# FFN up projections: one 512-column product of the high weights with both parts of the activation

## The chip, the cores and the metric

The kernel runs on one core of a Trainium2 chip, as one program in one launch. The metric is device time in microseconds (us) from start to end of that program. TensorE (PE in the profile) multiplies, VectorE (DVE) and ScalarE (ACT) do the elementwise work, and SyncE (SP) issues the DMA transfers. TensorE reads SBUF and writes PSUM, a memory of eight banks that hold 512 float32 columns each.

## What is computed

Two blocks over 256 tokens of 1024 features, all in float32. The first block has two layers, one with an mLSTM mixer and one with causal attention, each followed by a convolutional feed-forward net (FFN) with 2816 hidden features. The second block has two layers of convolution and sparse attention. The change lies in the FFN, which runs twice:

```
def conv_ffn(x, norm_g, w_up, conv_w, conv_b, w_down):
    u = rmsnorm(x, norm_g) @ w_up                 # 1024 -> 2 * 2816
    up = jnp.pad(u, ((0, 0), (CONV_W - 1, 0), (0, 0)))
    c = conv_b + up[:, 0:s_] * conv_w[0]
    for j in range(1, CONV_W):                    # 3 taps over the tokens
        c = c + up[:, j:j + s_] * conv_w[j]
    val, gate = jnp.split(c, 2, axis=-1)
    return (jax.nn.silu(gate) * val) @ w_down
```

## The kernel before

**Split products.** A float32 operand is split exactly into a high and a low part: ACT writes the high part (line 435), DVE subtracts it to get the low part (line 448). A product of two split operands is three matmul passes into the same PSUM columns: high by high (line 569), high by low (line 570), low by high (line 571). The first operand of a pass is stationary, 128x128 weights that are loaded ahead of the pass; the second is streamed through, one column per token.

**The FFN.** The hidden features go in 22 chunks of 128, each with a value half and a gate half. `up(j)` reads a 1 MB chunk of up weights (two loads of 512 KB) and computes, with features on the partitions, two blocks of 128x256: `gemm_pair` puts them in the two halves of one PSUM bank, 8 contraction steps of three passes each. For the first two chunks (HEAD) the products start from activations without the norm's factor. Then ACT scales each block from PSUM with the last tap, DVE adds the other two taps (two SCALAR_TENSOR_TENSOR each, also reading PSUM), ACT takes the silu of the gate, DVE multiplies, and the result is split again. `down(j - 2)` follows `up(j)` in the program; it takes 24 passes of 256 columns in the first FFN, and 12 of 512 columns (activation stationary, weights streamed) in the second. Four PSUM banks hold the down sums for the whole FFN; the other four serve everything else.

**Other work in the FFNs.** The modulation of the second block (`ada`) is a matrix-vector product on DVE: 48 chunks of 512 KB, each one SCALAR_TENSOR_TENSOR over 128x1024 with an accumulator (line 453). It is spread in the program over 38 of the 44 chunks.

**The order.** All instructions are recorded in program order. A planner in the kernel then goes through time with its own table of durations and fixes the order of each engine: the first in the program among those that are ready and whose buffers have room. On the chip each engine works through its list in that order. Buffers come from pages: 24 pages R of 1024 columns for split operands (a weight part takes a whole page, an activation part a quarter), 25 pages F for the rest.

**The convolution's mean in the second block.** In each layer of it, four small matmuls (line 1237) sum the taps, ACT copies the sums, and they go to DRAM and back through DMA (`zscr`, lines 1242 and 1244). TensorE then has a product of that result with the constant `ones` in its list (124 rows, line 422), and what stands behind it waits.

Of the kernel before, what the change touches and what calls it, by code (L numbers as in the profile page):

```python
# [20 lines left out]
EPS = 1e-6  # L21
# [20 lines left out]
for _n, _c in CONSTS:  # L42
# [4 lines left out]
# pages of on-chip memory: name -> (columns, dtype, count)  # L47
PAGES = {
    "R": (1024, F32R, 24),
# [4 lines left out]
# buffers: name -> (page, part of a page, columns)  # L54
POOLS = {
    "w": ("R", 4, 1024),
    "r": ("R", 1, 256),
# [10 lines left out]
SLOT_LAT = 200.0  # L68
WARM = 4096 / 1.2
# [23 lines left out]
class Buf:  # L93
    """A slot of a pool from its first to its last use, or a tile of its own (ap given)."""
# [41 lines left out]

class Op:
# [3 lines left out]
class Program:  # L141
    """Records the kernel's instructions in order, then fixes the order in which each engine issues its own:
    the first in the program among those whose operands and buffers are ready."""
# [39 lines left out]
    @staticmethod  # L183
    def spread(ops, p0, p1):
        """Gives ops the priorities of the program's positions p0..p1."""
        for i, op in enumerate(ops):
            op.prio = p0 + (p1 - p0) * (i + 0.5) / len(ops)

    def order(self, slots):
        """slots: page name -> list of tiles. Returns the ops in the planned order, with table loads."""  # L190
# [30 lines left out]
        # the place for a buffer: an opened page with the least room if it is a small one, else a whole page  # L221
# [54 lines left out]
        while left:  # L276
# [43 lines left out]
            for b in op.new:  # L320
# [7 lines left out]
                o = o * 256 if size < 4 else 0  # L328
# [53 lines left out]
def build(ctx, tc, a):  # L382
# [57 lines left out]
    # has the activation table ready for what comes after x  # L440
# [70 lines left out]
    # the part of FIRST that begins at each of n columns, then of the next  # L511
# [7 lines left out]
    hold = [None]  # L519

    def split_w(raw, n):
        hi, lo = new("w", n), new("w", n)
        op = act(hi, raw, AF.Copy)
        if hold[0]:
            pg.after(op, hold[0])
        tt(lo, raw, hi.f32, ALU.subtract)
        return hi, lo

    class Chunk:
        """k blocks k0..k1 of a chunk of weights; split, or as it is (native) for a float32 product; cuts: in pieces."""  # L530

        def __init__(self, dram, kc, mc, k0=0, native=False, cuts=None):
            self.mc, self.kp, self.k0 = mc, 1024 // mc, k0
            self.parts = []
            for k in range(k0, kc, self.kp):
                n = min(self.kp, kc - k) * mc
                raw = new("raw", n)
                if cuts:
                    hi, lo = new("w", n), new("w", n)
                    for c in cut(cuts, n):  # L540
                        load(raw[:, c], dram[:, k * mc + c.start:k * mc + c.stop])
                        act(hi[:, c], raw[:, c], AF.Copy)
                        tt(lo[:, c], raw[:, c], hi[:, c].f32, ALU.subtract)
                    self.parts.append((hi, lo))
                    continue
                load(raw, dram[:, k * mc:k * mc + n])
                self.parts.append((raw, None) if native else split_w(raw, n))

        def at(self, k, c0, c1):
            hi, lo = self.parts[(k - self.k0) // self.kp]  # L550
            o = ((k - self.k0) % self.kp) * self.mc
            return hi[:, o + c0:o + c1], lo and lo[:, o + c0:o + c1]

    def split_x(src):
        hi, lo = new("r"), new("r")
        act(hi, src, AF.Copy)
        tt(lo, src, hi.f32, ALU.subtract)
        return hi, lo

    # a product of split operands: high*high + high*low + low*high  # L560
    def mm3(out, lhs, rhs, start, stop, check=True):
        (lh, ll), (rh, rl) = lhs, rhs[:2]
        if ll is None:
            return mm(out, lh, rhs[2], start, stop, check=check)
# [19 lines left out]
    # tokens t of x (stationary) by weights w, token-major  # L584
    def mm_tm(out, x, w, t, start, stop):
        c = slice(t * 128, t * 128 + 128)
        if w[1] is None:
            mm(out, x[2][:, c], w[0], start, stop, check=False)
        else:
            mm3(out, (x[0][:, c], x[1][:, c]), w, start, stop, check=False)  # L590
# [6 lines left out]
    def gemm_tm(out, ws, xs, t):  # L597
        n = len(ws)
        for k in range(n):
            xh, xl = xs[k][:2]  # L600
            c = slice(t * 128, t * 128 + 128)
            mm3(out, (xh[:, c], xl[:, c]), ws[k], k == 0, k == n - 1)
# [17 lines left out]
    # 1 / sqrt(ms) for a few columns, with a Newton step  # L620
# [10 lines left out]
    # sums over partitions of the squares; n blocks are added before  # L631
# [13 lines left out]
    def scaled(xs, gname, i0):  # L645
        out = []
        for k, x in enumerate(xs):
            hi, lo = new("r"), new("r")
            gk = pcols(gname, i0 + k) if gname else an[:, k:k + 1]
            act(hi, x, AF.Copy, scale=gk)  # L650
            stt(lo, x, gk, hi.f32, ALU.mult, ALU.subtract)
            out.append((hi, lo))
# [10 lines left out]
    # products of zeros while the first operands arrive, for the tensor engine's clock  # L663
# [5 lines left out]
    # ================= mLSTM mixer =================  # L669
    # The norm's factor r of a token is left out of the products here: q and the value of h do not depend on it,  # L670
# [797 lines left out]
```

## Time and profile before

| | |
|---|---|
| Time, median of 3 runs | 874.43 us (873.71 to 876.65) |
| Profiled execution, first to last instruction (span) | 873.5 us |
| TensorE matmuls | busy 859.4 us, 98% |
| VectorE | busy 731.6 us, 84% |
| ScalarE | busy 559.4 us, 64% |
| Chain of waits | 95% TensorE |
| TensorE's clock, mean over the span | 0.995 of full speed |

For the profiled execution no other time is given than its span, which lies 0.9 us under the median. The busy time of an engine is the time in which at least one of its instructions is under way. Matmuls overlap: one of 256 columns is listed with some 283 ns, and the next begins 120 ns after it. What a pass costs on a busy TensorE is the distance between starts, not the listed duration. On DVE and ACT neighbours overlap too, by less.

The first FFN lies at about 118 to 322 us, the second at about 446 to 600 us. The second block's layers follow, to the end.

### The profile page before, as it was taken

Reading aid. Unit: us, or ns where it says so; the run is one execution under the profiler, and the core shown is the slowest. Engines: PE = TensorE matmul, PEld = TensorE weight load, DVE = VectorE, ACT = ScalarE, POOL = GpSimd, SP = SyncE. Lnnn points to the kernel's source line nnn. Section 1 sums busy time; section 2 is a strip of 40 time slices with the busy share of each in tenths; the row PEclk is TensorE's granted clock in tenths of the full one; section 3 lists DMA queues with packets and bytes.
Section 4 is the critical chain, followed back from the end, with each engine's and each line's share of the span. In section 5 each row is a group of like instructions: output and inputs, shape, how many; then the busy total and the mean of one; then the engine's idle time right before and its main releaser. Section 6 shows DMA issues by size and latency. Waiting matters only on the chain.

```text
span 873.5 us, 16714 instructions
## 1 busy us (share of the span) xinstructions
PE 859.4 (98%) x6270; PEld 804.2 (92%) x6270; DVE 731.6 (84%) x1677; ACT 559.4 (64%) x1170; POOL 0.2 (0%) x4
## 2 busy tenths in 40 slices
PE   8999999999999999999999999999999999998997
PEld 8999999999999999999989999998998858997866
DVE  6757899899977699987899986675799898798895
ACT  6846577545555496874776546556953797952883
POOL 0000000000000000000000000000000000000000
PEclk9999999999999999999999999999999999999999
DMA  8987766989865354478369985642340177440101
GB/s 317 408 307 228 257 201 200 322 293 319 295 219 179 111 192 134 138 252 301 121 204 355 349 282 175 192 122 86 123 143 13 27 237 302 134 125 13 58 16 49
DMA packets 50409, 170.33 MB, mean 195 GB/s; under 512 B 5860, under 2 KB 8428, under 8 KB 50328
## 3 DMA queue, kind: packets, MB, share of 16 engines
q1 hardware_dynamic: 50184, 169.26, 56.8%
q8 instruction: 49, 0.80, 0.4%
q14 instruction: 32, 0.26, 0.1%
q10 hardware_dynamic: 144, 0.00, 0.0%
HBM read 167.88 MB, written 1.37 MB: 194 GB/s over the span
## 4 chain that ended last, share of the span: by engine, by line
PE 95%; DMA 2%; ACT 1%; DVE 1%; SPq 0%; issue 0%; DVEq 0%; ACTq 0%
PE ps L569 26%; PE ps L570 26%; PE ps L571 26%; PE ps L422 14%; PE ps L426 2%; DMA F<-zscr 1%; PE ps L580 1%; ACT F L435 1%; DMA F<-in_a_w_v_dram 1%; DVE F L453 0%; DMA zscr<-F 0%; ACT R L435 0%; DVE R L448 0%; SPq L1244 0%; PE ps L1237 0%
## 5 line engine op out<-in xcount | busy, mean ns | idle before, releaser
L569 PE MATMUL ps<-R,R 128*128 128x256 f32 (+3 forms) x1788 | 531.8, 297 | 1.3 <-ACT R L435 1.2
L570 PE MATMUL ps<-R,R 128*128 128x256 f32 (+3 forms) x1788 | 522.8, 292 | 0.5 <-DVE R L448 0.5
L571 PE MATMUL ps<-R,R 128*128 128x256 f32 (+3 forms) x1788 | 522.5, 292 | 0.0
L448 DVE TENSOR_TENSOR R<-F,R 128x1024 fp32r<-128x1024 f32 (+4 forms) x339 | 324.3, 983 | 42.0 <-ACT R L435 31.3
L569 PEld LDWEIGHTS ps<-R,R 128*128 128x128 f32 x1788 | 343.5, 192 | 10.2 <-ACT R L435 2.3
L570 PEld LDWEIGHTS ps<-R,R 128*128 128x128 f32 x1788 | 343.7, 192 | 6.8 <-DVE R L448 1.2
L571 PEld LDWEIGHTS ps<-R,R 128*128 128x128 f32 x1788 | 343.4, 192 | 5.7 <-DVE R L448 0.5
L435 ACT ACTIVATE R<-F 128x1024 fp32r<-128x1024 f32 (+4 forms) x339 | 283.1, 864 | 30.6 <-DVE F L448 24.0
L422 PE MATMUL ps<-F,F 128*128 128x256 f32 (+6 forms) x568 | 128.9, 378 | 0.9 <-ACT F L435 0.8
L435 ACT ACTIVATE F<-ps 128x256 f32<-128x256 f32 (+3 forms) x197 | 70.6, 389 | 78.3 <-PE ps L571 37.7
L422 PEld LDWEIGHTS ps<-F,F 128*128 128x128 f32 (+2 forms) x568 | 89.9, 190 | 19.6 <-issue 8.9
L435 ACT ACTIVATE F<-ps,par 128x256 f32<-128x256 f32 (+1 forms) x84 | 42.3, 552 | 93.7 <-PE ps L571 93.3
L453 DVE SCALAR_TENSOR_TENSOR F<-ps,par,F 128x255 f32<-128x255 f32 (+1 forms) x160 | 66.0, 475 | 30.7 <-ACT F L435 30.7
L453 DVE SCALAR_TENSOR_TENSOR F<-F,par,F 128x256 f32<-128x256 f32 (+11 forms) x146 | 66.5, 463 | 1.2 <-ACT F L435 1.2
L435 ACT ACTIVATE F<-F 128x256 f32<-128x256 f32 (+2 forms) x120 | 46.7, 413 | 29.7 <-DVE F L453 17.8
L453 DVE SCALAR_TENSOR_TENSOR F<-F,F 128x1024 f32<-128x1024 f32 x48 | 58.0, 1217 | 0.0
L453 DVE SCALAR_TENSOR_TENSOR F<-F,par 128x255 f32<-128x255 f32 (+14 forms) x126 | 57.8, 460 | 0.0
L448 DVE TENSOR_TENSOR F<-ps,F 128x256 f32<-128x256 f32 (+2 forms) x80 | 32.8, 439 | 21.6 <-PE ps L571 16.2
L435 ACT ACTIVATE F<-F,s 128x128 f32<-128x128 f32 (+1 forms) x80 | 33.3, 445 | 4.9 <-DVE s L474 3.8
L435 ACT ACTIVATE R<-F,par 128x256 fp32r<-128x256 f32 x32 | 14.3, 505 | 28.9 <-DVE F L448 28.9
L1364 ACT ACT_TABLE_LOAD x23 | 29.5, 1283 | 0.4
L426 PE MATMUL ps<-con,F 128*128 128x128 f32 (+2 forms) x158 | 29.4, 271 | 0.1
(96 smaller groups left out, 370.9 us busy)
## 6 DMA issues: line engine op xcount, KB each, us to landing
F<-in_f_w_up_dram SPq DMA_DIRECT2D x88, 512.0 KB, 5.3
F<-in_w_ada_dram SPq DMA_DIRECT2D x48, 512.0 KB, 5.1
F<-in_f_w_down_dram SPq DMA_DIRECT2D x44, 512.0 KB, 5.9
F<-in_w_u_dram SPq DMA_DIRECT2D x16, 512.0 KB, 5.3
F<-in_w_out_dram SPq DMA_DIRECT2D x16, 512.0 KB, 3.8
F<-in_a_w_o_dram SPq DMA_DIRECT2D x8, 512.0 KB, 10.2
F<-in_a_w_out_dram SPq DMA_DIRECT2D x8, 512.0 KB, 10.2
F<-in_w_k_dram SPq DMA_DIRECT2D x8, 512.0 KB, 5.3
```

Of the source, the lines that this page charges most:

```text
L422: pg.add("PE", dur, lambda: nc.tensor.matmul(g(out), g(lhsT), g(rhs), start=start, stop=stop, skip_group_check=not check), [lhsT, rhs], [out])
L426: pg.add("PE", 110.0, lambda: nc.tensor.transpose(g(out), g(x), g(idn)), [x, idn], [out])
L435: nc.scalar.activation(g(out), g(x), func, bias=g(bias), scale=g(scale), **kw)
L448: return pg.add("DVE", ddur(n or x.n), lambda: nc.vector.tensor_tensor(g(out), g(x), g(y), op), [x, y], [out])
L453: nc.vector.scalar_tensor_tensor(g(out), g(x), g(s), g(y), op0, op1, **kw)
L569: nc.tensor.matmul(o, g(lh), g(rh), start=start, stop=False, **kw)
L570: nc.tensor.matmul(o, g(lh), g(rl), start=False, stop=False, **kw)
L571: nc.tensor.matmul(o, g(ll), g(rh), start=False, stop=stop, **kw)
L580: nc.tensor.matmul(g(out[e * 64:e * 64 + 64, c]), g(v[s][e]), g(p[e][:, r]), start=s == 0, stop=s == 1, skip_group_check=True)
L1364: nc.scalar.preload_act_table_set(TABLE[op[1]])
```

## The change

In the FFN's up projections of chunks 2 to 21, in both FFNs, the first two passes of each contraction step become one: the high weights are stationary, and the activation's high and low part are streamed as one operand of 512 columns, whose result fills a whole PSUM bank. The third pass (low weights by the high activation) adds into the bank's first half. The second half (high by low) is copied to SBUF by ACT, and DVE adds it to the first half, into SBUF, from where the taps read. So each chunk uses two banks, one per block.

For this the two parts of a split operand lie side by side in one buffer: 12 pages R of 2048 columns take the place of 24 of 1024, and a weight buffer holds both parts (1024 columns each), an activation buffer too (256 each). In the planner's table a pass costs 13.5 ns beside its columns where it was 3 ns; this holds for all split products, in the whole kernel.

```diff
 PAGES = {
-    "R": (1024, F32R, 24),
+    "R": (2048, F32R, 12),
 POOLS = {
-    "w": ("R", 4, 1024),
-    "r": ("R", 1, 256),
+    "w": ("R", 4, 2048),
+    "r": ("R", 1, 512),
...
+PASS = 13.5
...
+class Sp:
+    def __init__(self, v, o=0, n=None, x=None):
+        self.v, self.o, self.h, self.x = v, o, v.buf.cols // 2, x
...
+    @property
+    def both(self):
+        o, n, h = self.o, self.n, self.h
+        return V(self.v.buf, fn=lambda a: a.rearrange("p (e c) -> p e c", e=2)[:, :, o:o + n], iv=[(o, o + n), (h + o, h + o + n)])
...
     def mm3(out, lhs, rhs, start, stop, check=True):
...
-        pg.add("PE", 3 * (max(rh.n, 256) / 2.4 + 3), emit, [lh, ll, rh, rl], [out])
+        pg.add("PE", 3 * (max(n, 256) / 2.4 + PASS), emit, [lh, ll, rb], [out])
+    def mm2(out, lhs, rhs, start, stop):
+        lh, ll, rh, rb = lhs.hi, lhs.lo, rhs.hi, rhs.both
+        def emit():
+            nc.tensor.matmul(g(out), g(lh), g(rb), start=start, stop=False, skip_group_check=True)
+            nc.tensor.matmul(g(out[:, 0:256]), g(ll), g(rh), start=False, stop=stop, skip_group_check=True)
+        pg.add("PE", 768 / 2.4 + 2 * PASS, emit, [lh, ll, rb], [out])
+    def gemm_sums(ch, xs):
+        out = []
+        for b in range(2):
+            ps, lo, u = psum(), blk(), blk()
+            for k in range(8):
+                mm2(ps, ch.at(k, b * 128, b * 128 + 128), xs[k], k == 0, k == 7)
+            act(lo, ps[:, 256:512], AF.Copy)
+            tt(u, ps[:, 0:256], lo, ALU.add)
+            out.append(u)
+        return out
...
         def up(j):
-            ps = gemm_pair(Chunk(a["f_w_up"][l * NFF + j], 8, 256), xg if j < HEAD else xs)
+            ch = Chunk(a["f_w_up"][l * NFF + j], 8, 256)
+            if j < HEAD:
+                ps = gemm_pair(ch, xg)
+            else:
+                us = gemm_sums(ch, xs)
...
             for b in (1, 0):
-                u, f, c = half(ps, b), b * NFF + j, blk()
+                f, c = b * NFF + j, blk()
                 if j < HEAD:
                     u = blk()
                     tt(u, half(ps, b), r, ALU.mult)
+                else:
+                    u = us[b]
```

The rest of the diff passes split operands as one object in place of a pair. In the order rows below, `x4` at a row's end counts equal neighbours, and the numbers behind `_` name buffers.

TensorE's list in the first FFN before, where one contraction step of a chunk follows another (stationary weights `R`, second operand the activation part, bank `ps_152`):

```order
L571 MATMUL ps_152<-R_77,R_79 128x256
L569 MATMUL ps_152<-R_66,R_63 128x256
L570 MATMUL ps_152<-R_66,R_63 128x256
L571 MATMUL ps_152<-R_66,R_79 128x256
L569 MATMUL ps_152<-R_84,R_73 128x256
L570 MATMUL ps_152<-R_84,R_73 128x256
L571 MATMUL ps_152<-R_84,R_70 128x256
```

TensorE's list at the same place of the changed kernel, where block 0 ends and block 1 begins:

```order
L618 MATMUL ps_144<-R_70,R_65 128x512
L619 MATMUL ps_144<-R_70,R_65 128x256
L618 MATMUL ps_140<-R_68,R_64 128x512
L619 MATMUL ps_140<-R_68,R_64 128x256
...
L618 MATMUL ps_140<-R_70,R_65 128x512
L619 MATMUL ps_140<-R_70,R_65 128x256
```

Three passes of 256 columns have become one of 512 and one of 256, and each block has a bank of its own (`ps_144`, `ps_140`).

DVE's list before, one chunk of the first FFN in the stretch with `ada` (`mod`: an `ada` product; `R` with 128x1024: the low part of weights; 128x255 and 128x254: the taps; 128x256: gate times value, and its low part):

```order
L448 TENSOR_TENSOR F_91<-F_91,F_111 128x256
L453 SCALAR_TENSOR_TENSOR F_90,mod_167<-F_90,F_96 128x1024
L448 TENSOR_TENSOR R_64<-F_91,R_64 128x256
L453 SCALAR_TENSOR_TENSOR F_103,mod_167<-F_103,F_96 128x1024
L448 TENSOR_TENSOR R_68<-F_109,R_72 128x1024
L448 TENSOR_TENSOR R_63<-F_101,R_65 128x1024
L453 SCALAR_TENSOR_TENSOR F_91<-ps_156,par,F_91 128x255 x2
L453 SCALAR_TENSOR_TENSOR F_91<-ps_156,par,F_91 128x254 x2
L448 TENSOR_TENSOR R_76<-F_92,R_79 128x1024
```

DVE's list of the changed kernel, one chunk of the same stretch (the sum of the other block stands just ahead of the `ada` product that precedes the first row):

```order
L485 TENSOR_TENSOR R_64<-F_89,R_64 128x256
L490 SCALAR_TENSOR_TENSOR F_89<-F_87,par,F_89 128x255
L485 TENSOR_TENSOR R_66<-F_77,R_66 128x1024
L485 TENSOR_TENSOR F_89<-ps_143,F_87 128x256
L490 SCALAR_TENSOR_TENSOR F_89<-F_87,par,F_89 128x254
L485 TENSOR_TENSOR R_69<-F_80,R_69 128x1024
L490 SCALAR_TENSOR_TENSOR F_87<-F_89,par,F_87 128x255
L490 SCALAR_TENSOR_TENSOR F_96,mod_155<-F_96,F_84 128x1024
L490 SCALAR_TENSOR_TENSOR F_87<-F_89,par,F_87 128x254
L485 TENSOR_TENSOR R_71<-F_88,R_71 128x1024
L485 TENSOR_TENSOR F_87<-F_89,F_87 128x256
L485 TENSOR_TENSOR F_87<-ps_145,F_89 128x256
```

The same five 128x1024 instructions per chunk and four taps are there, two sums that read PSUM (`ps`) have come in, and the taps stand apart from each other, between the other work.

TensorE's list before, in the first layer of the second block, from the tap sums (`par`) to the product that waits for `zscr` (`con`); between the shown rows stand 69 passes of 256 columns in all:

```order
L1237 MATMUL ps_154<-F_104,par 32x256
L1237 MATMUL ps_154<-F_106,par 32x256 x2
L569 MATMUL ps_153<-R_78,R_65 128x256
...
L571 MATMUL ps_155<-R_66,R_76 128x256
L422 MATMUL ps_152<-F_101,con 128x256
```

TensorE's list of the changed kernel, the same piece, with 63 passes:

```order
L1297 MATMUL ps_140<-F_98,par 32x256
L1297 MATMUL ps_140<-F_94,par 32x256 x2
L606 MATMUL ps_145<-R_71,R_70 128x256
...
L608 MATMUL ps_144<-R_72,R_69 128x256
L459 MATMUL ps_146<-F_89,con 128x256
```

Six passes fewer lie between the two here; in the second layer it is 63 in place of 66.

## Rows read from the trace of the kernel before

**Rows 1.** The page: busy time by engine, and the chain of waits by engine.

```profile
PE 859.4 (98%) x6270; PEld 804.2 (92%) x6270; DVE 731.6 (84%) x1677; ACT 559.4 (64%) x1170; POOL 0.2 (0%) x4
PE 95%; DMA 2%; ACT 1%; DVE 1%; SPq 0%; issue 0%; DVEq 0%; ACTq 0%
```

**Rows 2.** Windows of the two FFNs: stretch, busy us by engine, clock, DMA.

```profile
143.00:243.00 100.00, 100.00 (x835) 100.00 (x835) 92.68 (x148) 55.13 (x82) 0.00 (x0) 1.00 0.89 303
243.00:318.00 75.00, 75.00 (x624) 74.80 (x623) 55.89 (x100) 44.61 (x83) 0.00 (x0) 1.00 0.51 165
446.00:496.00 50.00, 50.00 (x349) 46.83 (x348) 47.18 (x73) 32.28 (x54) 0.00 (x0) 1.00 0.92 333
496.00:546.00 50.00, 50.00 (x354) 47.05 (x353) 38.40 (x63) 27.25 (x43) 0.00 (x0) 1.00 0.74 245
```

**Rows 3.** TensorE's timeline, first FFN, passes of 256: start, duration, line.

```profile
169.82 0.28 PE L570 MATMUL ps<-R,R 128*128 128x256 f32 x1
...
171.98 0.28 PE L570 MATMUL ps<-R,R 128*128 128x256 f32 x1
```

**Rows 4.** TensorE's timeline, second FFN: twelve passes of 512 between passes of 256.

```profile
549.40 0.28 PE L571 MATMUL ps<-R,R 128*128 128x256 f32 x1
549.52 0.40 PE L569 MATMUL ps<-R,R 128*128 128x512 f32 x1
549.76 0.40 PE L570 MATMUL ps<-R,R 128*128 128x512 f32 x1
...
552.27 0.28 PE L569 MATMUL ps<-R,R 128*128 128x256 f32 x1
552.38 0.28 PE L570 MATMUL ps<-R,R 128*128 128x256 f32 x1
```

**Rows 5.** DVE and ACT groups by shape: count, busy us, mean ns, idle before.

```profile
L448 DVE TENSOR_TENSOR R<-F,R 128x1024 fp32r<-128x1024 f32 x230 | 276.2, 1218 | 22.1 <-ACT R L435 13.6 <-issue 7.8 <-PE ps L571 0.3
L453 DVE SCALAR_TENSOR_TENSOR F<-ps,par,F 128x255 f32<-128x255 f32 x80 | 34.9, 477 | 30.7 <-ACT F L435 30.7
L448 DVE TENSOR_TENSOR F<-ps,F 128x256 f32<-128x256 f32 x72 | 28.0, 419 | 18.6 <-PE ps L571 13.2 <-PE ps L426 2.0 <-ACT F L435 1.6
L435 ACT ACTIVATE F<-ps 128x256 f32<-128x256 f32 x102 | 35.6, 382 | 65.3 <-PE ps L571 35.0 <-PE ps L422 21.5 <-PE ps L426 8.0
L435 ACT ACTIVATE F<-ps,par 128x256 f32<-128x256 f32 x80 | 40.8, 561 | 93.7 <-PE ps L571 93.3 <-ACT R L435 0.4
L435 ACT ACTIVATE F<-F,par 128x256 f32<-128x256 f32 x16 | 9.3, 592 | 0.0
```

**Rows 6.** DVE's timeline in the first FFN: start, duration, what.

```profile
171.74 1.65 DVE L453 SCALAR_TENSOR_TENSOR F<-ps,par,F 128x255 f32<-128x255 f32 x4 [0.64 <-ACT F L435]
173.31 1.21 DVE L448 TENSOR_TENSOR R<-F,R 128x1024 fp32r<-128x1024 f32 x1
174.44 0.41 DVE L448 TENSOR_TENSOR F<-F,F 128x256 f32<-128x256 f32 x1
174.78 1.55 DVE L448 TENSOR_TENSOR R<-F,R 128x1024 fp32r<-128x1024 f32 x2
176.25 1.21 DVE L453 SCALAR_TENSOR_TENSOR F<-F,F 128x1024 f32<-128x1024 f32 x1
...
177.39 1.21 DVE L448 TENSOR_TENSOR R<-F,R 128x1024 fp32r<-128x1024 f32 x1
```

**Rows 7.** ACT's timeline: the blocks of one chunk and of the next.

```profile
170.69 1.02 ACT L435 ACTIVATE F<-ps,par 128x256 f32<-128x256 f32 x2 [3.00 <-PE ps L571]
...
179.32 1.02 ACT L435 ACTIVATE F<-ps,par 128x256 f32<-128x256 f32 x2 [3.01 <-PE ps L571]
```

**Rows 8.** TensorE's timeline where it waits for `zscr`, second block, both layers.

```profile
667.76 0.67 PE L422 MATMUL ps<-F,con 124*128 124x256 f32 x2 [1.35 <-DMA F<-zscr]
...
798.12 0.67 PE L422 MATMUL ps<-F,con 124*128 124x256 f32 x2 [3.05 <-DMA F<-zscr]
```

More of the change, by code (lines that the diff above doesn't have):

```diff
@@ L538, in __init__ @@
                 if cuts:
[L539 removed]
+                    w = Sp(new("w"), 0, n)
                     for c in cut(cuts, n):
                         load(raw[:, c], dram[:, k * mc + c.start:k * mc + c.stop])
[L542 to L544 removed]
+                        act(w[c].hi, raw[:, c], AF.Copy)
+                        tt(w[c].lo, raw[:, c], w[c].hi.f32, ALU.subtract)
+                    self.parts.append(w)
                     continue
                 load(raw, dram[:, k * mc:k * mc + n])
[L547 removed]
+                self.parts.append(Native(raw) if native else split_w(raw, n))
         def at(self, k, c0, c1):
[L550 removed]
             o = ((k - self.k0) % self.kp) * self.mc
[L552 removed]
+            return self.parts[(k - self.k0) // self.kp][o + c0:o + c1]
     def split_x(src):
[L555 to L558, printed above, removed]
+        x = Sp(new("r"))
+        act(x.hi, src, AF.Copy)
+        tt(x.lo, src, x.hi.f32, ALU.subtract)
+        return x
     def mm3(out, lhs, rhs, start, stop, check=True):
[L562 to L564 removed]
+        if isinstance(lhs, Native) or isinstance(rhs, Native):
+            return mm(out, lhs.x, rhs.x, start, stop, check=check)
+        n = rhs.n
+        lh, ll, rh, rl, rb = lhs.hi, lhs.lo, rhs.hi, rhs.lo, rhs.both
         def emit():
@@ L585, in mm_tm @@
     def mm_tm(out, x, w, t, start, stop):
[L586 to L590, printed above, removed]
+        mm3(out, x[t * 128:t * 128 + 128], w, start, stop, check=False)
     def gemm_fm(out, ws, xs):
@@ L647, in scaled @@
         for k, x in enumerate(xs):
-            hi, lo = new("r"), new("r")
+            o = Sp(new("r"))
             gk = pcols(gname, i0 + k) if gname else an[:, k:k + 1]
-            act(hi, x, AF.Copy, scale=gk)
-            stt(lo, x, gk, hi.f32, ALU.mult, ALU.subtract)
-            out.append((hi, lo))
+            act(o.hi, x, AF.Copy, scale=gk)
+            stt(o.lo, x, gk, o.hi.f32, ALU.mult, ALU.subtract)
+            out.append(o)
         return out
@@ L1059, in __init__ @@
             self.l, self.h, self.r = l, h, [None, None]
-            self.hi, self.lo, self.x = ([new(p) for _ in range(2)] for p in ("w", "w", "raw"))
+            self.hl, self.x = ([new(p) for _ in range(2)] for p in ("w", "raw"))
             self.xs = []
@@ L1150, in dsa_layer @@
         lat = [psum() for _ in range(2)]
-        cq = [(new("r"), new("r")) for _ in range(2)]
+        cq = [Sp(new("r")) for _ in range(2)]
         kix, kvT, ws = blk(), blk(), small(16)
@@ L1204, in dsa_layer @@
         t0 = len(pg.ops)
-        sm = [new("r", 128), new("r", 256)]
+        sm = new("r")
+        sm = [sm[:, 0:128], sm[:, 128:384]]
         for t, lo, hi in ((1, 128, 384), (0, 0, 128)):
```

52 lines of the change are left out of this document (32 added, 20 removed).

## Prediction

> **What bounds the kernel now.** I read the page first, for the engine that the chain of waits runs through: it is TensorE with 95% of the span, and TensorE is busy for 98% of it [rows 1]. Next come the windows of the two FFNs, since the change lies there: TensorE is busy for all of every stretch, so nothing that it waits for costs time there; DVE is busy for 92.7 of 100 us between 143 and 243 us, 94% between 446 and 496 us, and about 75% in the later part of either FFN [rows 2]. So TensorE's own passes set the pace, with DVE close behind in the early parts. The timeline of TensorE then gives the price of a pass. In the first FFN 18 starts lie between 169.82 and 171.98 us, which makes 120 ns a pass of 256 columns [rows 3]. In the second FFN, from 549.40 to 552.38 us, there are twelve passes of 512 columns and two of 256; less 2 x 120 ns, that is 2.74 us / 12 = 228 ns a pass [rows 4], against 240 ns for two passes of 256. Last, DVE's and ACT's timelines and groups by shape give the price of what is added, and the one place in the second block where TensorE's list is stopped by a transfer [rows 8] comes from looking for its waits.
>
> **What TensorE saves.** A contraction step takes 3 x 120 = 360 ns now and 228 + 120 = 348 ns with the change, so it saves 12 ns. There are 20 chunks in each of 2 FFNs, 2 blocks in each and 8 steps in a block: 640 steps, and 640 x 12 ns = 7.7 us. All of it lies on the path, because TensorE is never idle in these stretches. The bounds: the passes that change width come out at 240 ns (a 512 behind a 256, 549.52 to 549.76) and 110 ns (a 256 behind a 512, 552.27 to 552.38) [rows 4]. With 230 + 110 a step saves 20 ns, 12.8 us in all; with 240 + 120 it saves nothing. In the change every pass is such a neighbour. The starts are rounded to 10 ns, and the run as a whole has both changes in it, so I take its mean, 12 ns.
>
> What the array streams stays the same, 768 columns a step; one weight load and one start of a pass go. The Trainium skill, "TensorE: Matmul & The Clock Gate", section "Back-to-back issue gap", gives the distance of isolated matmuls as columns / 2.4 + 2.5 ns. By that rule the start of a pass costs 2.5 ns, and the estimate from the page is 640 x 2.5 ns = 1.6 us. The trace does not agree for this kernel's passes: 120 ns against the rule's 109 for 256 columns [rows 3].
>
> **What DVE and ACT gain in work.** 80 blocks get one ACT copy from PSUM (382 ns) and one DVE sum of PSUM and SBUF (419 ns) [rows 5]. That is 80 x 0.382 = 31 us more on ACT and 34 us more on DVE by listed durations. The scaling on ACT now reads SBUF, 592 against 561 ns [rows 5], 2.5 us more in all. ACT is busy for 55% in the first stretch [rows 2] and waits 3 us for TensorE in each chunk [rows 7], so for ACT TensorE is the cover.
>
> DVE needs a closer look, in its stretch of 143 to 243 us. One chunk lasts 8.63 us (170.69 to 179.32) [rows 7]; that is 72 passes of 120 ns. By starts, an instruction over 1024 columns takes 1.14 us (176.25 to 177.39), the four taps 1.57 us (171.74 to 173.31) and a 256-column one 0.34 us (174.44 to 174.78) [rows 6]. A chunk with two `ada` products has five of the first, the taps, and two of the last: 5.70 + 1.57 + 0.68 = 7.95 us, 92% of 8.63, which is what the window shows. With two sums more it is 8.63 us. TensorE's chunk becomes 8.63 - 16 x 0.012 = 8.44 us. So in this stretch DVE has slightly more to do than TensorE gives it time for, 0.2 us a chunk over some 11.6 chunks: 2.3 us that it falls behind. In the second FFN the chunk is 48 + 12 passes, 48 x 0.12 + 12 x 0.228 = 8.50 us before and 8.30 after; over the 6 chunks of 446 to 496 us DVE falls behind by 6 x 0.33 = 2.0 us. Later in either FFN a chunk without `ada` is 2.28 us lighter and DVE catches up.
>
> I cost this at nothing, since TensorE does not read what DVE has just made. Of the 12 pages for split operands, activations take about three, and nine hold weights, three chunks' worth at three pages each; so low parts can stand more than a chunk (8.4 us) ahead of their use. And the taps of chunk j feed `down(j)`, which comes after `up(j+2)`, two chunks later. A lag of 2.3 us fits in both. If that cover were gone, the two lags would be the cost, 4.3 us. PSUM has four banks beside the down sums; a chunk now takes two, each given back after the copy and the sum instead of after scaling and taps, so two chunks fit.
>
> Queued behind each new sum on DVE are the low parts of weights and `ada`; on ACT the high parts stand behind the copy. Both wait for TensorE's end of the block, as the scaling does now. SP's transfers keep their sequence in the FFN; the early stretches load the DMA engines to 0.89 and 0.92, against 0.51 once the first FFN's `ada` chunks are through [rows 2], so a transfer that is late there is first of all one of `ada`, whose products only the end of the second FFN reads.
>
> **What the planner moves.** Its new price of a pass changes lists in the whole kernel. The place that I can price: between the tap sums and the product that waits for `zscr`, 63 passes stand in either layer where it was 69 and 66. TensorE waits there already, 1.35 and 3.05 us [rows 8], so passes that leave this gap leave it open: 9 x 0.12 = 1.1 us lost. Elsewhere I see swaps in the attention and the second block but no wait that comes or goes; bounds are a gain or a loss of what TensorE waits there today, 4.4 us, and I take zero.
>
> **The sum.** 873.5 - 7.7 + 1.1 = 866.9 us of span. The median of the runs lies 0.9 us above the profiled span, so 867.8 us.
>
> **The rivals.**
> - A. DVE's lag reaches TensorE: the 4.3 us are paid and 867.8 becomes 872.1 us, the pace of 8.63 us being nearly that of today. For it: the sum of 8.63 against 8.44. Against it: the pages' lead, and that TensorE shows no idle time today with DVE at 93% [rows 2].
> - B. Slower than before: DVE instructions that wait for each other no longer overlap. The taps now stand apart, each reading what ACT or DVE has just written. By listed durations (1.218, 0.477 and 0.419) a chunk is 5 x 1.22 + 4 x 0.48 + 4 x 0.42 = 9.7 us, 1.26 us over TensorE's in 11.6 chunks and 1.4 us in 6: 23 us, of which one chunk of lead hides 8.5. 867.8 + 14.5 = 882 us. It decides from a DVE chunk of 8.63 us on, by as much as it is above. Against it: today's neighbours on DVE start 70 to 80 ns before the listed end of the one ahead [rows 6], whatever they are. The Trainium skill, "VectorE: DVE Perf Modes", section "The DRAIN you can't avoid", speaks for B: there the next instruction on DVE begins only when the pipe has emptied. The trace agrees only in part, since the rows show an overlap of 70 to 80 ns.
> - C. The change does not do what it says on TensorE: alternating widths pay 240 + 120 ns, and a step saves nothing. The single 240 in the trace [rows 4] speaks for it; the 110 behind and the mean of 228 speak against it. 874.4 + 1.1 = 875.5 us; with a start that costs only some ns, nearer 874.
> - D. The new lists cost or give something that I did not price, by up to the 4.4 us of waits there today: 863.4 to 872.2 us.
>
> **How the numbers follow.** My forecast of 867.8 us (866 to 870 by itself) has 0.58, A 0.12, B 0.07, C 0.06, D 0.17, of which I put two thirds on the costly side. What a measurement can tell from no change is 0.3%, or 2.6 us: faster is under 871.8, slower over 877.1. Forecast, four fifths of D and half of A (a lag that is paid in part) are faster, 0.78; half of A, a fifth of D and C are the same, some 0.14; B, with the upper tail of C, is slower, 0.08. The range of 863.4 to 873.0 us takes in the forecast, D and A; B, C and the tails are outside.
>
> **What would show it.** In the profile after: 640 passes of 512 columns more, starts in the first FFN that repeat with 348 ns a step; if 360, C. TensorE busy throughout the FFN windows with DVE at 98% or more from 143 to about 240 us; idle time of TensorE in front of a pass there, released by DVE's low parts or by a down product's operand, is A or B, told apart by DVE's sum per chunk (8.6 or 9.7 us). `ada` products would end later in the FFN than now. Waits for `zscr` of about 2.1 and 3.4 us instead of 1.35 and 3.05. The forecast is wrong if the FFNs together are not 6 to 9 us shorter, or if the rest of the kernel moves by more than 2 us.

## The result, and the profile after

The changed kernel takes 888.47 us (median of 4 runs, 887.48 to 890.57) against 874.1 us for the kernel before on the same chip: a ratio of 1.0162, 95% interval 1.0139 to 1.0186. I had forecast 867.8 us. The profiled execution has a span of 885.8 us where it was 873.5, so 12.3 us have to be found (the medians are 14.4 us apart).

Cut at five instructions of TensorE that both kernels have, the span divides like this (us):

| stage | before | after | difference |
|---|---|---|---|
| start, up to the first FFN | 116.7 | 116.7 | 0.0 |
| first FFN | 196.7 | 194.8 | -1.9 |
| attention | 104.7 | 108.1 | +3.4 |
| second FFN, up to the second block's first tap sums | 239.2 | 236.4 | -2.8 |
| second block: from there to layer 1's tap sums | 129.0 | 138.7 | +9.7 |
| from there to the end | 87.2 | 91.0 | +3.8 |

The change gives back 4.7 us where it was made, and 17 us are lost where no product has changed. The page of the changed kernel says the same: TensorE's share of the chain of waits has fallen from 95% to 82% [rows 1].

```profile
PE 862.2 (97%) x5630; PEld 774.3 (87%) x5630; DVE 762.3 (86%) x1757; ACT 589.5 (67%) x1250; POOL 0.2 (0%) x4
PE 82%; DVE 8%; ACT 4%; DMA 3%; issue 2%; SPq 0%; DVEq 0%; ACTq 0%
```

There are 640 instructions fewer on TensorE, and 80 more each on DVE and ACT, as the change says. TensorE's busy time is nonetheless 2.8 us longer, which fewer instructions cannot explain; the clock below does for the most part (6.8 us more, less the 4.5 us that the FFNs save, leaves 2.3).

**The FFNs.** TensorE's timeline of the changed kernel, one chunk of the first FFN: its first step, its last pass, and the first pass behind it.

```profile
181.23 0.40 PE L618 MATMUL ps<-R,R 128*128 128x512 f32 x1
181.47 0.28 PE L619 MATMUL ps<-R,R 128*128 128x256 f32 x1
...
186.76 0.28 PE L619 MATMUL ps<-R,R 128*128 128x256 f32 x1
186.88 0.28 PE L606 MATMUL ps<-R,R 128*128 128x256 f32 x1
```

Sixteen steps from 181.23 to 186.88 us are 353 ns each, against 360 before [rows 3] and 348 forecast. By the mean distance between starts in this FFN the wide pass takes 236 ns and the narrow one 117. The wide one is 8 ns dearer than among its like in the second FFN's down product [rows 4]. A step saves 360 - 353 = 7 ns, and 640 x 7 ns = 4.5 us, beside the 4.7 us that the table shows for the two FFN stages.

The windows of the changed kernel that answer to [rows 2]; after the stretch and its length come PE, PEld, DVE, ACT and POOL busy, the granted clock and the DMA share.

```profile
143.00:243.00 100.00, 100.00 (x665) 91.61 (x664) 99.45 (x168) 64.71 (x104) 0.00 (x0) 1.00 0.85 294
446.00:496.00 50.00, 50.00 (x258) 41.53 (x257) 49.44 (x82) 35.83 (x63) 0.00 (x0) 1.00 0.82 285
496.00:546.00 50.00, 50.00 (x264) 42.63 (x263) 45.10 (x79) 32.98 (x55) 0.00 (x0) 1.00 0.79 286
```

DVE is full, as forecast, and TensorE still has no idle time. DVE's timeline of the changed kernel, the same place in two neighbouring chunks of the stretch with `ada`:

```profile
178.38 1.22 DVE L485 TENSOR_TENSOR R<-F,R 128x1024 fp32r<-128x1024 f32 x1
...
186.99 1.23 DVE L485 TENSOR_TENSOR R<-F,R 128x1024 fp32r<-128x1024 f32 x1
```

That is 8.61 us a chunk, where the forecast had 8.63, beside 8.53 us for TensorE (16 x 0.353 + 24 x 0.12).

**Outside the FFNs** TensorE waits at places where it did not. The waits of TensorE in the changed kernel from 600 us on: line, releaser, us in total, times, longest.

```profile
PE ps L463 <- ACT s L472: 3.2, 1, 3.2
PE ps L459 <- issue: 2.7, 1, 2.7
PE ps L1297 <- DVE F L490: 2.3, 2, 1.2
PE ps L459 <- DMA F<-zscr: 1.8, 1, 1.8
```

The second and the fourth are the product of the mean that waits for `zscr`, 2.70 and 1.78 us where it was 3.05 and 1.35 [rows 8]. (The row that says "issue" is the same instruction in layer 1; the profile sees no releaser for it, and the runs with a later mean below show that the transfer ends it.) The first and the third are new: 3.2 us in front of the transposes of layer 1's latent rows, and 1.05 and 1.24 us in front of the last tap sums of either layer. In the attention there are three more:

```profile
PE ps L463 <- DVE F L485: 3.0, 3, 1.9
```

Behind the waits the clock falls. Windows of the changed kernel, columns as above:

```profile
668.00:671.40 3.40, 3.40 (x15) 3.27 (x16) 2.51 (x7) 0.00 (x0) 0.00 (x0) 0.53 0.00 0
746.00:751.00 5.00, 1.80 (x9) 1.25 (x7) 4.38 (x15) 4.87 (x17) 0.00 (x0) 0.91 0.31 84
751.00:757.00 6.00, 5.63 (x24) 5.10 (x22) 5.26 (x9) 5.35 (x14) 0.00 (x0) 0.51 0.86 289
757.00:763.00 6.00, 6.00 (x34) 5.51 (x34) 4.25 (x5) 5.43 (x13) 0.00 (x0) 1.00 0.23 79
808.00:811.40 3.40, 3.40 (x17) 3.31 (x16) 2.88 (x8) 0.00 (x0) 0.00 (x0) 0.52 0.00 0
```

After the waits that end at 667.9, 750.4 and 807.7 us TensorE runs at the lower of its two levels (1.2 GHz of 2.4) for 3.4, 6.8 and 3.4 us. TensorE's timeline shows what a pass of 256 columns costs there:

```profile
808.50 0.41 PE L607 MATMUL ps<-R,R 128*128 128x256 f32 x1
808.71 0.41 PE L608 MATMUL ps<-R,R 128*128 128x256 f32 x1
```

210 ns from start to start, not 120. 13.6 us at half speed lose 6.8 us. The kernel before has no such stretch behind its two waits; its window behind the longer one shows the full clock:

```profile
798.00:802.00 4.00, 3.88 (x26) 3.73 (x27) 3.18 (x9) 0.66 (x2) 0.00 (x0) 1.00 0.00 0
```

**The sum.** FFNs -4.5. Attention: waits +3.0. Layer 0: waits 1.05 + 3.2 + (1.78 - 1.35) = +4.7, clock 10.2 / 2 = +5.1. Layer 1: waits 1.24 + (2.70 - 3.05) = +0.9, clock +1.7. Together 10.9 of 12.3 us; of the rest, 1.2 us lie in layer 1, and I have no row for them.

**Where the longest wait comes from.** It is in ACT's order. ACT's timeline of the changed kernel, then of the kernel before, around the same two instructions: a scaling that makes features of the first token half (`mod`), and the third of the four squares for the norm of layer 0's output in the second half (128x256 from `ps`).

```profile
744.06 0.79 ACT L472 ACTIVATE F<-ps,mod 128x128 f32<-128x128 f32 x2
...
745.20 0.37 ACT L472 ACTIVATE F<-ps 128x256 f32<-128x256 f32 x1
```

```profile
737.02 0.38 ACT L435 ACTIVATE F<-ps 128x256 f32<-128x256 f32 x1 [0.18 <-PE ps L571]
...
738.33 0.79 ACT L435 ACTIVATE F<-ps,mod 128x128 f32<-128x128 f32 x2
```

Before, all four squares stand ahead of the features. Now two do (738.72 and 739.07 us), and the last two stand behind all of them. DVE's timeline of the changed kernel shows what this delays: the update of the second half waits for that norm, and the rows to be transposed are written behind it on DVE's list.

```profile
746.62 1.68 DVE L490 SCALAR_TENSOR_TENSOR F<-F,s,F 128x256 f32<-128x256 f32 x4 [0.77 <-ACT s L472]
...
749.77 0.48 DVE L496 TENSOR_SCALAR F<-ps,s 128x256 f32<-128x256 f32 x1
```

TensorE's timeline, changed kernel first, shows what follows:

```profile
746.82 0.37 PE L608 MATMUL ps<-R,R 128*128 128x456 f32 x1
750.39 0.87 PE L463 MATMUL ps<-con,F 128*128 128x128 f32 x3 [3.20 <-ACT s L472]
751.63 3.78 PE L459 MATMUL ps<-F,F 128*128 128x128 f32 x16 [0.37 <-DVE F L496]
```

```profile
744.14 0.37 PE L571 MATMUL ps<-R,R 128*128 128x456 f32 x1
744.35 1.95 PE L422 MATMUL ps<-F,F 128*128 128x128 f32 x16
```

Before, the last pass of 456 columns is followed at once by the 16 products of the second half's features, since its norm is ready. Now that norm is late, and TensorE stands for 3.2 us in front of the transposes. The profile names an instruction of ACT (`s`) as the releaser, which ends 0.09 us ahead of them; the DVE instruction above, which writes what the first two of them read, ends 0.14 us ahead. Then TensorE takes 3.78 us for the same 16 products that took 1.95: the wait is paid, and then the clock. No run moved these squares alone, so their place on the list is read from the rows, not tried. The kernel before with nothing but the new price (below) has the same order: there the third square starts at 746.71 us, behind the last features (745.56).

### The profile page after: what moved, and what is told of

Read it like the earlier page. It is cut to its first block, busy times and chain, and to the rows that moved or that the text cites. A ratio compares the mean times of both kernels' runs of the same rounds, so it can differ in the third digit from the quotient of the medians.

```text
span 885.8 us, 15574 instructions
## 1 busy us (share of the span) xinstructions
PE 862.2 (97%) x5630; PEld 774.3 (87%) x5630; DVE 762.3 (86%) x1757; ACT 589.5 (67%) x1250; POOL 0.2 (0%) x4
## 4 chain that ended last, share of the span: by engine, by line
PE 82%; DVE 8%; ACT 4%; DMA 3%; issue 2%; SPq 0%; DVEq 0%; ACTq 0%
PE ps L618 17%; PE ps L606 14%; PE ps L607 14%; PE ps L608 14%; PE ps L459 13%; PE ps L619 8%; DVE F L490 3%; ACT F L472 2%; PE ps L463 2%; DVE R L485 2%; ACT R L472 1%; DMA F<-zscr 1%; DVE F L520 1%; DMA F<-in_b_w_o_dram 1%; DVE s L517 1%
## 5 line engine op out<-in xcount | busy, mean ns | idle before, releaser
L485 DVE TENSOR_TENSOR R<-F,R 128x1024 fp32r<-128x1024 f32 (+4 forms) x339 | 329.4, 986 | 38.0 <-ACT R L472 35.4
L606 PE MATMUL ps<-R,R 128*128 128x256 f32 (+3 forms) x1148 | 351.6, 306 | 1.1 <-ACT R L472 1.1
L607 PE MATMUL ps<-R,R 128*128 128x256 f32 (+3 forms) x1148 | 342.1, 298 | 0.7 <-DVE R L485 0.7
L608 PE MATMUL ps<-R,R 128*128 128x256 f32 (+3 forms) x1148 | 341.9, 298 | 0.0
L606 PEld LDWEIGHTS ps<-R,R 128*128 128x128 f32 x1148 | 221.1, 193 | 11.5 <-ACT R L472 2.6
L618 PE MATMUL ps<-R,R 128*128 128x512 f32 x640 | 227.8, 399 | 0.0
L607 PEld LDWEIGHTS ps<-R,R 128*128 128x128 f32 x1148 | 221.2, 193 | 6.7 <-DVE R L485 1.6
L608 PEld LDWEIGHTS ps<-R,R 128*128 128x128 f32 x1148 | 220.9, 192 | 5.7 <-DVE R L485 0.4
L619 PE MATMUL ps<-R,R 128*128 128x256 f32 x640 | 179.7, 281 | 0.0
L472 ACT ACTIVATE F<-ps 128x256 f32<-128x256 f32 (+3 forms) x277 | 100.7, 386 | 85.3 <-PE ps L608 38.0
L618 PEld LDWEIGHTS ps<-R,R 128*128 128x128 f32 x640 | 120.3, 188 | 29.5 <-issue 0.9
L619 PEld LDWEIGHTS ps<-R,R 128*128 128x128 f32 x640 | 120.9, 189 | 0.5
L490 DVE SCALAR_TENSOR_TENSOR F<-F,par 128x255 f32<-128x255 f32 (+28 forms) x246 | 107.1, 469 | 5.2 <-ACT F L472 4.6
L490 DVE SCALAR_TENSOR_TENSOR F<-F,par,F 128x254 f32<-128x254 f32 (+11 forms) x186 | 86.7, 476 | 4.9 <-ACT F L472 4.1
L485 DVE TENSOR_TENSOR F<-ps,F 128x256 f32<-128x256 f32 (+2 forms) x160 | 66.2, 430 | 27.0 <-PE ps L608 19.7
L472 ACT ACTIVATE F<-F,par 128x256 f32<-128x256 f32 x96 | 56.9, 598 | 18.6 <-DVE F L485 18.3
## 6 DMA issues: line engine op xcount, KB each, us to landing
F<-in_a_w_out_dram SPq DMA_DIRECT2D x8, 512.0 KB, 10.2
```

The source lines that it names most:

```text
L472: nc.scalar.activation(g(out), g(x), func, bias=g(bias), scale=g(scale), **kw)
L485: return pg.add("DVE", ddur(n or x.n), lambda: nc.vector.tensor_tensor(g(out), g(x), g(y), op), [x, y], [out])
L490: nc.vector.scalar_tensor_tensor(g(out), g(x), g(s), g(y), op0, op1, **kw)
L606: nc.tensor.matmul(o, g(lh), g(rh), start=start, stop=False, **kw)
L607: nc.tensor.matmul(o, g(lh), g(rl), start=False, stop=False, **kw)
L608: nc.tensor.matmul(o, g(ll), g(rh), start=False, stop=stop, **kw)
```

## The experiments

The theory after the comparison: the wide product does what was forecast, if less of it, and the loss is the planner's new order outside the FFNs, which two things can bring: the new price of a pass, and the new pages. The rivals: the wide product itself, with its work on DVE and ACT, brings the loss; or the clock alone does. Ratios are to the kernel before on the same chip, with 95% intervals.

**The price alone, taken back (in the changed kernel).**

```
-PASS = 13.5
+PASS = 3.0
```

> The changed kernel with the planner's old price of a pass (3 ns beside its columns in place of 13.5); the wide product and the double pages stay. The trace of the changed kernel puts the FFNs 1.8 and 2.8 us shorter than before, and everything after them longer: 3.3 us in the attention, 9.7 and 3.9 us in the second block's layers. T1, the price of a pass reorders these stages: about 870 us (874.1 - 4.6), and no new waits after the FFNs. T2, the pages of double width do it: about 887 us. T3, the wide product itself does it, by its two banks per chunk and its DVE sums: about 887 us.

881.4 us, 1.0066 (1.0046 to 1.0086). About 7 us come back, not all: attention 106.2, layer 0 132.5, layer 1 90.1 us.

**The price alone, put into the kernel before.**

```
-        pg.add("PE", 3 * (max(rh.n, 256) / 2.4 + 3), emit, [lh, ll, rh, rl], [out])
+        pg.add("PE", 3 * (max(rh.n, 256) / 2.4 + 13.5), emit, [lh, ll, rh, rl], [out])
```

> The kernel before with nothing but the planner's new price of a pass (13.5 ns). T1 (price): the loss outside the FFNs without the FFNs' gain, 874.1 + 16.9 = 891 us, or at least 882. T2 (pages) and T3 (wide product): 874 us.

889.49 us, 1.0164 (1.0141 to 1.0186): a loss as large as the whole from one number of the planner, with no instruction added, removed or made wider. Its stages are not all those of the changed kernel: layers 0 and 1 take 137.4 and 91.5 us, but the attention takes 103.6, less than before. The longest of its waits of TensorE from 600 us on are the ones seen above:

```profile
PE ps L422 <- DMA F<-zscr: 5.5, 2, 3.4
PE ps L426 <- DVE F L459: 2.9, 1, 2.9
PE ps L1237 <- DVE F L453: 2.2, 2, 1.2
```

**The pages alone** (old up projections, old price; activation and weight parts side by side in 12 wide pages; the edit is shown against the kernel before).

```
-    "R": (1024, F32R, 24),
+    "R": (2048, F32R, 12),
...
-    "w": ("R", 4, 1024),
-    "r": ("R", 1, 256),
+    "w": ("R", 4, 2048),
+    "r": ("R", 1, 512),
```

> The pages of double width alone: the changed kernel with the old up projections (three passes of 256, halves of one bank) and the old price of 3 ns. T1 (price) and T3 (wide product): 874 us. T2 (pages): 882 to 891 us.

891.6 us, 1.0192 (1.0174 to 1.0209). The pages alone also bring a loss as large as the whole, at other places: the first FFN 201.0 us with a wait of 2.1 us at 138, attention 109.9.

**Pages and price, without the wide product** (the changed kernel with the old up projections).

```
-            if j < HEAD:
-                ps = gemm_pair(ch, xg)
-            else:
-                us = gemm_sums(ch, xs)
+            ps = gemm_pair(ch, xg if j < HEAD else xs)
...
-                    u = us[b]
+                    u = half(ps, b)
```

> The changed kernel with the old up projections; pages of double width and the price of 13.5 ns stay. T1 (price): 885 to 891 us. T2 (pages): 885 to 891 us. T3 (wide product): 874 us. With the two kernels before it, this tells whether price and pages add up.

888.8 us, 1.0157 (1.0139 to 1.0174), the changed kernel's time. Price and pages do not add up (1.6 and 1.9% apart, 1.6% together): each draws another order. The wide product is not needed for the loss in the second block (137.4 and 91.3 us here). The attention takes 103.8 us without it, so the changed kernel's 3.4 us there are not brought by price and pages together. Waits of the same kind on DVE come without the wide product in the run before (3.1 us the longest), so they need not be its work, but no run separates what brings them in the changed kernel.

**The wide product alone, in nearly the old order** (the kernel before with the wide product; old weight pages and price, and the planner counts a step as three old passes, the copy and the sum as 1 ns; 30 of TensorE's rows outside the FFNs moved, against more than 400 in the changed kernel by its trace).

```
+    "r2": ("R", 2, 512),
...
+                pg.add("PE", 3 * (256 / 2.4 + 3), emit, [lh, ll, rb], [ps])
+            act(lo, ps[:, 256:512], AF.Copy).dur = 1.0
+            tt(u, ps[:, 0:256], lo, ALU.add).dur = 1.0
```

> The kernel before with the wide product alone: old pages (only the FFN's activation parts lie side by side), old price; the planner counts a step of the wide product as three old passes and the copy and the sum as 1 ns each, so that outside the FFNs TensorE's list is that of before but for 26 rows in the attention and 4 in the second block. T1 (the lists outside the FFNs make the loss): 874.5 - 4.5 (640 steps at 353 ns instead of 360, as the changed kernel's trace has them) = 870 us, 868 to 872. T3 (the wide product itself, with its DVE sums, delays what follows): above 877 us.

874.47 us (10 runs, 871.88 to 877.12), 0.9994 (0.9978 to 1.0010): the loss is gone, but the gain hardly shows, short of the 870 us expected. So the wide product's own work on DVE and ACT does not make the loss, in the attention (104.4 us) as little as in layer 0 (129.1): that rival falls. The FFN stages show -1.6 and -0.7 us, though a step takes 353 ns here too; 0.67 us of the difference is a wait for ACT at 441 us that the kernel before has not, and I have no row for the rest. Layer 1 takes 89.9 us where it was 87.2. Its windows there:

```profile
790.00:795.50 5.50, 1.65 (x14) 1.47 (x14) 3.37 (x9) 0.00 (x0) 0.00 (x0) 1.00 0.06 21
795.50:799.00 3.50, 3.50 (x15) 3.32 (x16) 2.27 (x7) 0.00 (x0) 0.00 (x0) 0.52 0.01 2
```

The wait for `zscr` has grown to 3.85 us, and the clock falls behind it.

**The same, passes grouped** (four steps' wide passes, then their four narrow ones).

```
+                    for k in range(k0, k0 + 4):
+                        nc.tensor.matmul(g(ps), g(ws[k][0]), g(xs[k][2]), start=k == 0, stop=False, skip_group_check=True)
+                    for k in range(k0, k0 + 4):
+                        nc.tensor.matmul(g(ps[:, 0:256]), g(ws[k][1]), g(xs[k][0]), start=False, stop=k == 7, skip_group_check=True)
```

> As the kernel before it, with the passes of four steps in another sequence: four of 512 columns, then four of 256, so that the width changes twice in eight passes. If a change of width is what costs 5 ns a step (236 + 117 in the changed kernel's trace against 228 + 120), a step comes to 348 ns and the time to 3 us under the kernel before it, 867 us; if it is the wide pass with this operand that is slow, the two are equal, 870 us.

870.59 us, 0.9950 (0.9935 to 0.9964). TensorE's timeline of this kernel, the second block of a chunk:

```profile
181.83 1.09 PE L619 MATMUL ps<-R,R 128*128 128x512 f32 x4
182.76 0.63 PE L621 MATMUL ps<-R,R 128*128 128x256 f32 x4
...
184.64 0.28 PE L570 MATMUL ps<-R,R 128*128 128x256 f32 x1
```

Eight steps in 2.81 us are 351 ns, and a wide pass among its like still takes 0.93 / 4 = 233 ns. So it is not the change of width that makes it dearer than 228. Both FFNs together are 6.0 us shorter than before (194.4 and 235.5). Layer 1 keeps its wait for `zscr` (3.45 us) and a clock fall, and layer 0 takes 130.9 us where it was 129.0. Of the 4.9 us between the two profiled spans 2.3 lie in the first stage, where no fall of the clock lies in this execution (114.3 us) and two in that of the kernel before.

**Is a low price good for the order, or was the old order a lucky one?** The kernel before with prices of 2 and of 5.

```
-        pg.add("PE", 3 * (max(rh.n, 256) / 2.4 + 3), emit, [lh, ll, rh, rl], [out])
+        pg.add("PE", 3 * (max(rh.n, 256) / 2.4 + 2), emit, [lh, ll, rh, rl], [out])
```

(and `+ 5` in the second)

> The kernel before with the planner's price of a pass at 2 ns instead of 3. Nothing is closer to or farther from the chip's 120 ns by more than 1 ns, but the list moves: 204 rows in the attention, 56 and 27 in the second block's layers. T1a (a price near the chip's own is what makes a bad list): 874 us, within 2. T4 (the list before is a lucky one, and nearly any other costs): 880 to 892 us.

> The kernel before with the planner's price of a pass at 5 ns instead of 3: 285 rows moved in the attention, 37 and 8 in the second block's layers. T1a (a price near the chip's own makes the bad list): a fifth of the way from 3 to 13.5, 875 to 878 us. T4 (the list before is a lucky one): 880 to 892 us.

878.23 us, 1.0039 (1.0024 to 1.0054), and 879.73 us, 1.0067 (1.0038 to 1.0096). Both neighbours of 3 are slower, with a wait of 2.1 us at 137 us that the kernel before has not. The time does not run with the price: price 3 with these pages is a favourable draw, and any edit that orders anew is likely to lose some of it. Neither expectation had it in this form.

**Is it the clock?** Constant products that change no output, placed ahead of the mean's product in layer 1 of the grouped kernel.

```
+            for _ in range((0, 7)[l]):
+                nc.tensor.matmul(g(mp), g(ones[0:124, :]), g(con[0:124, 0:256]), start=True, stop=True)
```

> The grouped kernel (870.6 us) with seven products of constants, 427 ns each, put directly ahead of the product that waits for the convolution's mean in the second block's last layer; nothing else moves in TensorE's list. The wait there is 3.45 us and the clock falls to half for 3.4 us after it. Clock theory: with the wait filled (3.0 of 3.45 us) the clock stays up, the layer is 1.7 us shorter, 868.9 us. If the wait is all that counts, 870.6 us; if the fillers hold up something, more.

870.86 us, 0.9944 (0.9924 to 0.9964): no gain over the grouped kernel. Layer 1 did go from 89.1 to 87.2 us, but in this execution the clock fell in layer 0, behind a wait of 1.90 us that was 1.72 us without a fall there.

**The wait removed instead:** in the grouped kernel the planner is told that `zscr` lands later, so that it lists more passes ahead of the mean's product.

```
-ZDUR, ZTAIL = 480.0, 4000.0
+ZDUR, ZTAIL = 480.0, 8000.0
```

> The grouped kernel with the planner's time for the transfer of the convolution's mean at 8 us instead of 4: the waiting product stands 20 rows later in TensorE's list in the first layer and 20 in the second, some 2.4 us each, and little else moves. If its waits (1.7 and 3.45 us) and the clock that falls after the second are lost time: 1.7 + 2.4 + 1.7 less, 865 us. If DVE's taps, which need the mean, set these layers: 870 us, since they start no earlier.

864.22 us (863.36 to 864.93), 0.9863 (0.9839 to 0.9887): faster than both kernels. All waits of TensorE from 600 us on in this kernel:

```profile
PE ps L423 <- ACT F L436: 0.7, 2, 0.4
PE ps L570 <- ACT R L436: 0.5, 1, 0.5
```

Both `zscr` waits are gone, layer 1 takes 84.0 us, and between 52 us and the last few us the clock does not fall.

**Which part of the order costs what, in the changed kernel.** The old price for the second block's layers alone:

```
+    late = [False]
...
-        pg.add("PE", 3 * (max(n, 256) / 2.4 + PASS), emit, [lh, ll, rb], [out])
+        pg.add("PE", 3 * (max(n, 256) / 2.4 + (3.0 if late[0] else PASS)), emit, [lh, ll, rb], [out])
...
+    late[0] = True
```

> The changed kernel (888.5 us) with the planner's old price of a pass in the second block's layers alone; start, FFNs and attention keep their lists. If the new price spoils the lists of these layers: they go from 138.7 and 91.0 us to the 129 to 132 and 88 to 90 that the kernels with the old price have, 876 to 882 us. If they are long because of the state in which the FFN leaves the engines: 888 us.

884.23 us, 1.0083 (1.0053 to 1.0112): a miss. Layer 0 takes 135.8 us and layer 1 89.4; the wait in front of the transposes is still 2.33 us. The price in those layers explains only part of their loss.

**The clock alone, in the changed kernel:** constant products at the three waits with a fall behind them, order unchanged.

```
+                    for _ in range(n):
+                        nc.tensor.matmul(g(tp[:, 0:256]), g(ones), g(con[:, 0:256]), start=True, stop=True)
...
+            for _ in range((4, 6)[l]):
+                nc.tensor.matmul(g(mp), g(ones[0:124, :]), g(con[0:124, 0:256]), start=True, stop=True)
```

> The changed kernel with products of constants (427 ns each) ahead of three instructions of TensorE's list at which it waits, and nothing moved: four ahead of the mean's product in the first layer (wait 1.8 us), seven ahead of the first transpose of the latent rows in the second layer (3.2 us), six ahead of the mean's product there (2.7 us). The clock is at half after these three waits for 3.4, 6.8 and 3.4 us. Clock theory: half of 13.7 us comes back, 881 to 883 us. If the waits alone make the loss: 888 us.

884.91 us, 1.0096 (1.0070 to 1.0122): 3.6 us come back, less than expected. The three falls are gone and both layers are shorter (136.1 and 89.4 us, 4.2 us together), but others came. The one near 46 us lasts twice as long in this execution (the first stage takes 118.3 us), and one is new in the attention, as this window shows:

```profile
329.00:333.00 4.00, 4.00 (x22) 4.00 (x23) 3.96 (x21) 1.17 (x5) 0.00 (x0) 0.57 0.00 0
```

Behind the filled place in layer 0 TensorE also waits 0.72 and 0.73 us for DVE, where the changed kernel waits 0.37 us once. Clock falls are part of the loss, not its whole.

**The later mean alone, with the wide product, and in the changed kernel:** the edit of `ZTAIL` in the kernel before, in the wide product in the old order, and in the changed kernel, on one chip.

> The kernel before with the planner's time for the mean's transfer at 8 us instead of 4, nothing else: the waiting product stands 14 rows later in the first layer and 18 in the second, the rest of TensorE's list is that of before. Its waits of 1.35 and 3.05 us should go: about 4.4 us less, 870.3 us. With it the wide product's own worth can be read where no such wait and no fall of the clock behind it mix in.

868.73 us, 0.9930 (0.9907 to 0.9954).

> The wide product in the old lists (874.5 us, no gain) with the same later place of the mean's product. If that kernel's gain in the FFNs (640 steps of 360 - 353 ns, 4.5 us) was eaten by the longer wait and the clock behind it: 866 to 867 us, some 4 us under the kernel before with the late mean. If the wide product gains nothing on the whole: 870 us, as that one.

867.78 us, 0.9915 (0.9892 to 0.9937). Against the run before it the alternating wide product is worth about 1 us in the medians, and the intervals overlap; the FFN stages show 2.3 us. The grouped kernel's interval with the later mean (0.9839 to 0.9887) lies below that of the kernel before with it: the grouped wide product is worth 0.7%.

> The changed kernel (888.5 us) with the same later place, 22 and 16 rows. If its waits for the mean (1.8 and 2.7 us) and the two falls of the clock behind them (1.7 us each) are a part of its loss that has nothing to do with the wide product: 4.5 + 3.4 less, 880.5 us. If the time only moves elsewhere: 886 to 888 us.

880.43 us, 1.0052 (1.0027 to 1.0077), as expected. The mean's waits and the falls behind them were some 8 of the 14 us by the medians, on two chips (1.1 of 1.6% by the ratios). What is left is the rest of the order: of TensorE's waits from 600 us on, the two that the comparison found new head the list.

```profile
PE ps L463 <- ACT s L472: 3.2, 1, 3.2
PE ps L1297 <- DVE F L490: 2.3, 2, 1.2
```

## Why the prediction was wrong

- **What bounds the kernel, TensorE in the FFNs: right.** TensorE stays busy there, and the change makes both FFNs shorter.
- **What TensorE saves: right in kind, mis-sized.** 7 ns a step and not 12: 4.5 us in place of 7.7. I took the wide pass from the second FFN's down product, where the weights are what is streamed; in the up projection it takes 233 to 236 ns, grouped or not. Why is open. Rival C, nothing saved, did not come.
- **What DVE and ACT gain in work: right.** 8.61 us a chunk against 8.63 forecast; DVE at 99.45 of 100 us; TensorE waits for neither engine inside the FFNs but for 0.30 us at 445 us. Neither rival A nor B happened. With 8.53 us for TensorE's chunk DVE falls behind by an estimated 0.08 us each, some 0.9 us in all, and no wait of TensorE shows it. `ada` does not end later in the first FFN, as I had said it would: its last product starts at 238.2 us where it was 243.9.
- **What the planner moves: this step failed.** "Elsewhere I see swaps in the attention and the second block but no wait that comes or goes; bounds are a gain or a loss of what TensorE waits there today, 4.4 us, and I take zero." The measured loss there is 17 us. Three things were wrong in it. The bound: waits of today bound what a new order can give, not what it can cost, since a new order makes waits where there were none. The reading: a swap on ACT's list (squares behind scalings) looks harmless beside TensorE's list, and decides when TensorE's next operand is ready. And the clock: a wait is paid again behind it, 6.8 of the 17 us, which no term had. The piece that I did price, six and three passes fewer in front of the mean's product, was worth next to nothing by itself: waits of 1.78 and 2.70 us, where 2.1 and 3.4 were forecast, against 4.40 us in all before. Both signs that the forecast named against itself came: the FFNs are 4.7 us shorter and not 6 to 9, and the rest moved by 17 us and not by 2.
- **The rivals.** D was the right mechanism with a size of 4.4 us, a quarter of what came, and it was given no way of ending slower than before. That pages of double width order anew by themselves was in no term; by itself this costs as much as the price does.

## What to carry to other kernels

Where a planner orders the whole program from a table of costs, changing one cost is a change to every stage: compare the timelines of all of them, and try the new table by itself, without the feature. A tuned order is one draw among many. Those that another price or other pages drew here came out 0.4 to 1.9% slower, and the one with the later mean alone 0.7% faster. So an edit that saves 0.5% must either leave the order alone or be given its own search; here the wide product paid once the order was kept, its passes were grouped, and the wait behind `zscr` was filled. On a list that nothing overtakes, look for the producer: an early consumer costs its wait, and on TensorE perhaps a stretch at half clock behind it.

## What the runs showed of the hardware that was not expected

- The granted clock fell to half behind waits of 1.78, 2.70, 3.20 and 3.85 us, and a pass of 256 columns then started 210 ns after the last. The length of the wait does not decide it alone: the kernel before waits 3.05 us at the same place [rows 8] and keeps the full clock behind it, and the grouped kernel waits 1.72 us in layer 0 without a fall where a wait of 1.90 us had one.
- Falls differ between executions of the same list: the changed kernel with and without the later mean has one and the same list on every engine up to the second block, and near 47 us one has 3.4 us at half clock, the other 6.8. The first stage takes 116.7 and 118.0 us. Over the runs of this case it takes 114.3 to 114.7 us in the three that have no fall in it, and up to 119.1 in the others.
- A fall can cost nothing: with the one near 330 us (constant products at the three waits) the attention takes 108.2 us, without it, in the changed kernel, 108.1, since two waits that follow (0.62 and 0.48 us) go.
- A pass of 512 columns takes 233 to 236 ns in one product and 228 in another; the page counts as many weight loads as passes (5630 of each).
